# One more pipe step between scores and turned weights in the differential attention of the prompt

## The chip, the cores and the metric

One core of one Trainium2 chip runs the kernel. It has five engines with a queue of their own each: TensorE (PE; its weight loads are a row of their own, PEld), VectorE (DVE), ScalarE (ACT), GpSimd (POOL) and SyncE (SP), which here starts nearly all DMA transfers. The metric is the device time of one execution in microseconds. Before the change it is 935.0 us, the median of three runs (934.97 to 935.01).

## The reference

One decoder layer for a prompt of 512 rows and a group of 8 x 4 sample rows. The part that matters here is the differential attention of the mixer: 4 heads, each with two 64-wide query and key components and a 128-wide value. The prompt attends to itself causally, the sample rows attend to a paged cache of 256 rows.

```python
def diff_attend(q, k, v, mask, lam):
    s = jnp.einsum('bqhcd,bkhcd->bhcqk', q, k) * (DA_QK_DIM ** -0.5)
    s = jnp.where(mask[None, None, None], s, -jnp.inf)
    p = jax.nn.softmax(s, axis=-1)
    a = p[:, :, 0] - lam * p[:, :, 1]
    return jnp.einsum('bhqk,bkhd->bqhd', a, v)
```

Around it stand an mLSTM head group that reads the same normalised rows, an output projection of both, cross-attention into 256 memory tokens and a gated MLP with a short convolution. All of it is in fp32, large products as a sum of three products of rounded high and low halves.

## The kernel before

The kernel is one Python function that issues instructions through a tile framework. A tile comes from a pool: `npool` (`N(...)`, 5 buffers of 1032 columns), `t2p` (`T2(...)`, 8 buffers of up to 562 columns), `zp` (3 of 512), and in PSUM `psm` (`mmp(...)`, 5 banks) and `psa` (`at(...)`, 3 banks). The framework's scheduler, when the program is built, decides the order of the instructions on every engine from the order of the code, the free buffers and its own estimate of durations; semaphores are put in by it. At run time each engine takes its instructions strictly in that order. An instruction that uses a buffer again waits for the last reader of the tile that had it before.

The stage around the change runs from about 244 to 300 us. Two passes are woven into each other there.

The *prompt pass* has 16 tiles: tile i is row block b = i // 4 and head h = i % 4, and has (b + 1) * 128 keys. `da_soft(i)` (L1248) makes the scores of the two components with PE into two PSUM tiles `sda` (L1257; L1258 adds the mask with a bf16 product), takes their negated maxima with VectorE (`nm`, L1260), the exponentials and their sums with ScalarE into the weight tile `pda` (L1261), the factors `rc` with VectorE (L1263, L1264), and joins the components with one VectorE update (L1265). `da_turn(i)` (L1268) transposes the weights with PE into `tpa` (L1273) and copies them with ScalarE to `aT` (L1275). `da_av(i)` (L1279) multiplies them with the values on PE into `oda` (L1285), which ScalarE scales into `dao` (L1287). `da_end(i)` (L1289) closes a row block after its fourth tile: square on ScalarE (`dasq`, L1099), sum on VectorE (`dass`, L1101), a power and a product on GpSimd, transposes on PE (`dat`, L1106), and so on. `pipe` (L375) runs these as stages of a pipeline: its generator `prompt` makes one step per `next`, and in step t it issues stage s for tile t - s, the last stage first.

The *sample pass* goes over 8 batches. For each, SyncE loads two pages of cached keys into `wst` (256 KB each), PE transposes them in two groups of four (`tpk`, L1229, tiles of `psa`), ScalarE copies the first group and VectorE the second to `kT` (L1230), and PE makes the scores `ssc` of a pair of batches (L1242). VectorE and ScalarE make maxima and exponentials of them (L1052, L1053). After all eight, `sample_softmax` sums them with PE (`spa`, L1072) and ScalarE copies the sum (`spc`, L1074). Then eight loads of cached values (`vt`) and the products `ops` (L1341) follow. `out_gate` (L1029) runs in between: it transposes the mLSTM rows (`mlt`, L1039), gates them with VectorE into `mltm` (tiles of `t2p`, L1045; the sample rows also into `xts`, L296), and ScalarE and GpSimd split them into halves (L146, L147).

The generator `prompt` is stepped by hand from the sample pass: once per step of the loop over the key batches (10 steps), twice within `sample_softmax`, three times in the loop over the values, once after it, and four times between the first steps of the output projection (`proj`, lines L411 to L413).

Of the kernel before, what the change touches and what calls it, by code (L numbers as in the profile page):

```python
# [15 lines left out]
P = 128  # L16
# [6 lines left out]
H = 4  # L23
# [54 lines left out]
def kernel(ctx: ExitStack, tc: tile.TileContext, I, O):  # L78
# [23 lines left out]
    def S(shape, dt, name):  # L102
        return sp.tile(list(shape), dt, name=name, tag="S")

    def N(name, w=1024):
        return npool.tile([P, 1032], F32, name=name, tag="N")[:, :w]

    def T2(shape, name, dt=F32):
        return t2p.tile(list(shape), dt, name=name, tag="T2")
# [7 lines left out]
    def mmp(name="mm"):  # L117
        return psm.tile([P, 512], F32, name=name, tag="mm")

    def small(w, name, p=P):  # L120
        return sm.tile([p, w], F32, name=name, tag=name)
# [87 lines left out]
    def stage():  # L209
        return stg.tile([P, 1024], F32, name="wst", tag="st")  # L210
# [164 lines left out]
    def pipe(n, *stages):  # L375

        for t in range(n + len(stages) - 1):
            for s in reversed(range(len(stages))):
                if 0 <= t - s < n:
                    stages[s](t - s)  # L380
            yield
# [148 lines left out]
    for b in range(2):  # L530
        kept.append(norm_turn(xms[b], P, "g_mem_src", memT, b * P))
        if b == 0:

            t = turned[0].ins
            fill = mmp("fill")
            for _ in range(NFILL):
                with burst(t):
                    t = mm(fill, lhsT=warm[:, 0:P], rhs=warm, start=True, stop=True).ins
# [132 lines left out]
    for c0, c1 in HALF:  # L671
# [5 lines left out]
        t = T2([64, n], "gt")  # L677
# [253 lines left out]
    for g in range(2):  # L931
        for h in range(0, H, 2):
            t = stage().rearrange("p (j b e) -> p j b e", j=2, b=4)
# [38 lines left out]
    t = None  # L972
    for h in range(H):
        with burst(t):
            t = mm(pg[NS * h:NS * h + NS, P:2 * P + 1], lhsT=sm_t[:, h, :], rhs=vNs[:, h, :], start=True, stop=True).ins
    for h in range(H):
        with burst(t):
            t = mm(pg[NS * h:NS * h + NS, 4:12], lhsT=qT[:, h, SEQ:], rhs=nT[:, h, :], start=True, stop=True).ins
    for b in range(NB):
        for h in range(H):  # L980
            with burst(t):
                t = mm(pi[NS * h:NS * h + NS, 0:P], lhsT=qzm[:, 256 * h + b * NS:256 * h + (b + 1) * NS],
                       rhs=csts[b // 4, h][:, b % 4, :], start=(b == 0), stop=(b == NB - 1)).ins
# [226 lines left out]
    for b in range(4):  # L1210
        c = slice(b * P, b * P + P)
# [3 lines left out]
    kst, kts, pts, aTs, outs, rcs = {}, {}, {}, {}, {}, {}  # L1215
# [32 lines left out]
    def da_soft(i):  # L1248
        b, h = i // H, i % H
        c0 = b * P  # L1250
        nk = c0 + P
        pt = pts[i] = N("pda").rearrange("p (c k) -> p c k", c=2)
        nm = small(2, "nm")
        su = small(2, "su")
        sv = [mmp("sda")[:, :nk] for _ in range(2)]
        for c in range(2):
            mm(sv[c], lhsT=(dqz if c else dqT)[:, h, c0:c0 + P], rhs=dkT[:, h, 0:nk], start=True, stop=False)  # L1257
            mm(sv[c][:, c0:nk], lhsT=identb, rhs=cmaskb, start=False, stop=True)  # L1258
        for c in range(2):
            VRED(out=nm[:, c:c + 1], in_=sv[c], axis=AX.X, op=MAX, negate=True)  # L1260
            ACT(out=pt[:, c, :nk], in_=sv[c], func=AF.Exp, bias=nm[:, c:c + 1], accum_out=su[:, c:c + 1])  # L1261
        rc = sm.tile([P, 2], F32, name="rc", tag="rc", bufs=6)
        nc.vector.reciprocal(out=rc, in_=su)  # L1263
        VTS(out=rc[:, 1:2], in0=rc[:, 1:2], scalar1=su[:, 0:1], scalar2=nlam, op0=MUL, op1=MUL)  # L1264
        STT(out=pt[:, 0, :nk], in0=pt[:, 1, :nk], scalar=rc[:, 1:2], in1=pt[:, 0, :nk], op0=MUL, op1=ADD)  # L1265
        rcs[i] = rc
# [28 lines left out]


    W.nslots = 0
    prompt = pipe(4 * H, da_soft, lambda i: None, da_turn, da_av, da_end)
    sall = S([P, NB, 260], F32, "das")
    nm, su = small(NB, "snm"), small(NB, "ssu")  # L1300
    for t, _ in enumerate(pipe(NB, dk_load, dk_turn, dk_scores)):
# [45 lines left out]
                           start=False, stop=True).ins  # L1347

    for t, _ in enumerate(pipe(NB, dv_load, lambda b: None, dv_out)):
        if t % 2 == 0 and t > 2:  # L1350
            next(prompt, None)
        F.run(2)
    oS = T2([P, P], "daoS")
# [156 lines left out]
    def mk_scores(bs):  # L1510

        t = None
        ps = {b: at("ssc")[:, :256] for b in bs}
        for e in range(2):
            if e and bs[0] == 0:
                next(prompt)
                t = scored[0].ins
            for b in bs:
                o = ps[b][:, e * P:e * P + P].rearrange("p (h c t) -> p h c t", h=2, c=2)
                for c in range(2) if b < 3 else (None,):  # L1520
                    for j in range(8):
                        g = NS * (j % 4)
                        if c is None:
                            w, k = o[g:g + NS], view(kst[b][0], 512 * e + NS * j, [(256, 2), (DM, 2), (1, NS)])
                        else:
                            w, k = o[g:g + NS, :, c], view(kst[b][c], 512 * e + NS * j, [(256, 2), (1, NS)])
                        with burst(t):
                            t = mm(w, lhsT=qx[e][j // 4][:, j % 4, b].rearrange("p e g t -> p (e g t)"), rhs=k,
                                   start=(j < 4), stop=(j >= 4)).ins
        for b in bs:  # L1530
            nc.scalar.copy(out=sc[:, b], in_=ps[b])
        return t
# [66 lines left out]
    def steps():  # L1599

        for t in range(11):
            if t == AHEAD:
                ch_soft(t)
                yield
            if 0 <= t - 3 < 8:
                ch_out(t - 3)
            if 0 <= t - 2 < 8:
                ch_turn(t - 2)
            if t < 8 and t != AHEAD:
                ch_soft(t)  # L1610
            yield

    prompt = steps()
# [15 lines left out]
    for b in range(0, NB, 2):  # L1629
        t = mk_scores((b, b + 1))  # L1630
# [219 lines left out]
    for gi, js in enumerate(groups):  # L1850
# [6 lines left out]
        nk = len(js)  # L1857

        def one(b, ps, i, s, cs=slice(0, 512)):
            t = act[i // 2][:, i % 2]  # L1860
            st, en = i == 0, i == nk - 1
            if b == 4:
                return sample_mm(ps, [acs[i], acs[i + 1]], s[1], i == 0, i == nk - 2)
            s = s[0]
            c0 = b * P
            mm(ps, lhsT=t[:, 0, c0:c0 + P], rhs=s[:, 0, i % 2, cs], start=st, stop=False)  # L1866
            if js[i] == 21:
                return mm(ps, lhsT=t[:, 0, c0:c0 + P], rhs=s[:, 1, i % 2, cs], start=False, stop=en)
            mm(ps, lhsT=t[:, 0, c0:c0 + P], rhs=s[:, 1, i % 2, cs], start=False, stop=False)  # L1869
            return mm(ps, lhsT=t[:, 1, c0:c0 + P], rhs=s[:, 0, i % 2, cs], start=False, stop=en)  # L1870
# [29 lines left out]
        if not last:  # L1900
            behind = []
            for n0 in (0, 512):
# [4 lines left out]
                for i in range(nk):  # L1907
# [3 lines left out]
                    for b in range(4):  # L1911
                        t = one(b, ps[b], i, s)
# [14 lines left out]
        def chunk(b, n0):  # L1927
            while len(wd) < (nk // 2 if n0 == 0 else nk):
                wd.append(W.get())
            w = 256 if (b, n0) == (TORD[-1], 512) else 512  # L1930
            for o in range(0, 512, w):
                ps = mmp()[:, :w]
                for i in range(0, nk, 2 if b == 4 else 1):
                    t = one(b, ps, i, wd[(n0 and nk // 2) + i // 2], slice(o, o + w))
                add_y(b, ps, n0 + o, w)
            return t
# [39 lines left out]
        t = chunk(TORD[1], 0)  # L1976

        for n0 in (0, 512):
            with burst(t.ins):
                t = chunk(TORD[0], n0)  # L1980
# [79 lines left out]
```

## Time and profile before

| | |
|---|---|
| median of three runs | 935.0 us |
| profiled execution | 934.94 us |
| its span | 933.2 us |
| PE, busy of the span | 912.8 us (98%) |
| VectorE | 607.1 us (65%) |
| ScalarE | 377.9 us (40%) |
| GpSimd | 224.6 us (24%) |
| DMA, mean over the span | 140 GB/s |

The span reaches from the first to the last recorded instruction; the time of an execution is 1.74 us longer. Busy times are sums over the records of one engine. A row of a timeline merges instructions of one kind that follow each other: its length reaches from the first's start to the last's end, and since an instruction begins before the one in front has wholly ended, two rows can overlap. In brackets stands the idle time of the engine ahead of the row and the instruction that ended it. The page's slices of the span show a busy PE throughout, while VectorE and ScalarE are fullest in slices 10 to 12 of 40, which is the stage of this change.

### The profile page before, as it was taken

The page shows a single profiled execution, that of the slowest core. Times are in us where ns is not written, and L with a number is a line of the kernel's source. Part 1 is how long each engine was busy: PE and PEld are TensorE (multiplying, and loading weights), DVE is VectorE, ACT ScalarE, POOL GpSimd, SP SyncE. Part 2 cuts the span into 40 slices and gives each one's busy share as a digit, 9 for nine tenths or more (in the row PEclk, how much of TensorE's full clock was granted, in tenths as well). Part 3 has the DMA queues.
Part 4 walks back from the last instruction along what each step waited for, and adds up shares of the span by engine and source line. Part 5 has one row for each costly group of instructions (what it writes and reads, how often), then busy time and mean ns, then how long its engine had stood idle before and what let it go on. Part 6 is the DMA issues. An engine that isn't in the chain of part 4 may idle for free. (4 is left out here: it accounts for less than half of the span.)

```text
span 933.2 us, 17471 instructions
## 1 busy us (share of the span) xinstructions
PE 912.8 (98%) x6780; PEld 797.2 (85%) x6780; DVE 607.1 (65%) x1128; ACT 377.9 (40%) x728; POOL 224.6 (24%) x475
## 2 busy tenths in 40 slices
PE   8999999999999999999999999999999999999995
PEld 5899787879866778999877899889888998999974
DVE  5845144565888338677645878537748775776767
ACT  5645233344587437724534532422212222222232
POOL 6611000034442126581000652001000110110114
PEclk9999999999999999999999999999999999999998
DMA  9950023335780439966777632152154304413023
GB/s 288 316 182 6 1 91 139 91 102 164 234 299 17 136 113 293 302 213 228 284 240 201 199 105 62 31 174 69 27 136 136 91 4 127 124 47 91 25 94 118
DMA packets 120834, 130.59 MB, mean 140 GB/s; under 512 B 8599, under 2 KB 86264, under 8 KB 120752
## 3 DMA queue, kind: packets, MB, share of 16 engines
q1 hardware_dynamic: 114568, 125.96, 42.8%
q10 hardware_dynamic: 6184, 3.53, 1.3%
q8 instruction: 53, 0.87, 0.4%
q14 instruction: 29, 0.24, 0.1%
HBM read 112.54 MB, written 16.93 MB: 139 GB/s over the span
## 5 line engine op out<-in xcount | busy, mean ns | idle before, releaser
L485 PE MATMUL mm<-fT,wslot 128*128 128x256 f32 x1872 | 235.9, 288 | 0.0
L485 PEld LDWEIGHTS mm<-fT,wslot 128*128 128x128 f32 x1872 | 234.4, 188 | 1.8 <-issue 0.8
L146 ACT CAST wslot<-wst 128x1024 fp32r<-128x1024 f32 x125 | 130.4, 1050 | 255.7 <-issue 72.7
L147 DVE TENSOR_TENSOR wslot<-wst,wslot 128x1024 fp32r<-128x1024 f32 x125 | 154.2, 1239 | 76.5 <-ACT wslot L146 74.6
L1866 PE MATMUL mm<-wslot,act 128*128 128x512 f32 (+1 forms) x180 | 69.4, 387 | 0.0
L1869 PE MATMUL mm<-wslot,act 128*128 128x512 f32 (+1 forms) x172 | 67.1, 391 | 0.0
L1870 PE MATMUL mm<-wslot,act 128*128 128x512 f32 (+1 forms) x172 | 66.8, 392 | 0.0
L1768 POOL COPY cvo<-u 128x2 f32<-128x2 f32 x43 | 10.4, 242 | 216.0 <-DVE u L1766 216.0
L411 PE MATMUL mm<-wslot,hT 128*128 128x512 f32 x128 | 51.3, 402 | 0.0
L413 PE MATMUL mm<-wslot,hT 128*128 128x512 f32 x128 | 51.0, 400 | 0.0
L485 PE MATMUL mm<-hT,wslot 128*128 128x256 f32 (+1 forms) x384 | 51.0, 289 | 0.0
L412 PE MATMUL mm<-wslot,hT 128*128 128x512 f32 x128 | 50.9, 397 | 0.0
L1763 DVE TENSOR_TENSOR u<-mm,rsb 128x256 f32<-128x256 f32 x43 | 18.1, 424 | 48.8 <-PE mm L485 48.7
L485 PEld LDWEIGHTS mm<-hT,wslot 128*128 128x128 f32 x384 | 49.2, 188 | 0.5 <-issue 0.2
L1866 PEld LDWEIGHTS mm<-wslot,act 128*128 128x128 f32 x180 | 34.3, 191 | 7.9 <-issue 0.4
L1870 PEld LDWEIGHTS mm<-wslot,act 128*128 128x128 f32 x172 | 32.3, 188 | 6.9 <-issue 0.4
L1869 PEld LDWEIGHTS mm<-wslot,act 128*128 128x128 f32 x172 | 32.3, 188 | 6.8
L1780 ACT ACTIVATE c<-c 128x560 f32<-128x560 f32 x21 | 14.1, 672 | 56.8 <-DVE c L1774 56.7
L1774 DVE SCALAR_TENSOR_TENSOR c<-u,cvT,c 128x560 f32<-128x560 f32 x43 | 34.3, 799 | 0.9
L1773 DVE SCALAR_TENSOR_TENSOR c<-u,cvT,c 128x560 f32<-128x560 f32 x43 | 34.1, 794 | 0.2
L1881 DVE TENSOR_TENSOR yp<-mm,yp 128x512 f32<-128x512 f32 (+1 forms) x41 | 27.1, 674 | 4.8 <-PE mm L1870 4.6
L413 PEld LDWEIGHTS mm<-wslot,hT 128*128 128x128 f32 x128 | 24.1, 188 | 5.0
(497 smaller groups left out, 1858.0 us busy)
## 6 DMA issues: line engine op xcount, KB each, us to landing
wst<-in_w_up_dram SPq DMA_DIRECT2D x42, 512.0 KB
wst<-in_w_in_dram SPq DMA_DIRECT2D x28, 512.0 KB
wst<-in_w_down_dram SPq DMA_DIRECT2D x20, 512.0 KB
kvt<-in_cache_mem_k_dram SPq DMA_DIRECT2D x10, 512.0 KB
kvt<-in_cache_mem_v_dram SPq DMA_DIRECT2D x10, 512.0 KB
wst<-in_w_mk_dram SPq DMA_DIRECT2D x8, 512.0 KB
xb<-in_x_prompt_dram SPq DMA_DIRECT2D x8, 512.0 KB
wst<-in_cache_dk_dram SPq DMA_DIRECT2D x16, 256.0 KB
```

The lines of the kernel that those rows point to most:

```text
L146: nc.scalar.copy(out=hi, in_=src)
L147: (eng or nc.vector).tensor_tensor(out=lo, in0=src, in1=f32(hi), op=SUB)
L411: mm(ps[b], lhsT=xt.hi(k, c0, c0 + n), rhs=s[:, 0, kk, :], start=(k == 0), stop=False)
L412: mm(ps[b], lhsT=xt.hi(k, c0, c0 + n), rhs=s[:, 1, kk, :], start=False, stop=False)
L413: return mm(ps[b], lhsT=xt.lo(k, c0, c0 + n), rhs=s[:, 0, kk, :], start=False, stop=(k == nk - 1))
L485: mm(ps[i], lhsT=s[:, l, k, :], rhs=x(k, c0, c1), start=(k == 0 and j == 0), stop=(k == 7 and j == 2))
L1773: STT(out=c, in0=u[:, 1:EXT - 1], scalar=w[1], in1=c, op0=MUL, op1=ADD)
L1774: STT(out=c, in0=u[:, 0:EXT - 2], scalar=w[0], in1=c, op0=MUL, op1=ADD)
L1866: mm(ps, lhsT=t[:, 0, c0:c0 + P], rhs=s[:, 0, i % 2, cs], start=st, stop=False)
L1869: mm(ps, lhsT=t[:, 0, c0:c0 + P], rhs=s[:, 1, i % 2, cs], start=False, stop=False)
L1870: return mm(ps, lhsT=t[:, 1, c0:c0 + P], rhs=s[:, 0, i % 2, cs], start=False, stop=en)
L1881: VTT(out=y, in0=ps, in1=y, op=ADD)
```

## The change

Between `da_soft` and `da_turn` the pipeline of the prompt pass had one empty stage and now has two, so that it has six stages and 21 steps instead of five and 20. The loop over the cached values steps it at t = 2, 4, 6 and 8 instead of 4, 6 and 8. And the weight tiles of row blocks 0 and 1 (128 or 256 keys) come from `t2p` with just the columns they need instead of from `npool`.

```diff
-        pt = pts[i] = N("pda").rearrange("p (c k) -> p c k", c=2)
+        pt = pts[i] = T2([P, 2, nk], "pda") if b < 2 else N("pda").rearrange("p (c k) -> p c k", c=2)
...
-    prompt = pipe(4 * H, da_soft, lambda i: None, da_turn, da_av, da_end)
+    prompt = pipe(4 * H, da_soft, lambda i: None, lambda i: None, da_turn, da_av, da_end)
...
-        if t % 2 == 0 and t > 2:
+        if t % 2 == 0 and t > 0:
             next(prompt, None)
```

The scheduler makes another order of this stage; from some 330 us on all engines' queues read as before. On PE at the start of the stage, behind the scores of tiles 0 and 1, there stood (the numbers are those of the tile's allocation; `tpk` of 2618, 2664, 2670, 2736 and 2742 are the key transposes of batches 0 to 2, `tpa_2697` is the turn of tile 0, `sda_2704` and `sda_2705` the scores of tile 2):

```order
L1229 MATMUL tpk_2618<-cpk_87,wst_2572 128x128 x4
L1229 MATMUL tpk_2664<-cpk_87,wst_2624 128x128 x4
L1229 MATMUL tpk_2670<-cpk_87,wst_2624 128x128 x4
L1229 MATMUL tpk_2736<-cpk_87,wst_2676 128x128 x4
L1229 MATMUL tpk_2742<-cpk_87,wst_2676 128x128 x4
L1039 MATMUL mlt_2777<-cpk_87,mlh_1377 128x128 x4
L1273 MATMUL tpa_2697<-cpk_87,pda_2593 128x128
L1257 MATMUL sda_2704<-dkT_1303,dqT_1304 128x128
```

and now stands (2700 and 2701 are the scores of tile 2, 2732 and 2738 the transposes of batch 2, `ssc` the scores of batches 1 and 0):

```order
L1257 MATMUL sda_2700<-dkT_1303,dqT_1304 128x128
L1258 LDWEIGHTS cb_114
L1258 MATMUL sda_2700<-cb_114 128x128
L1229 MATMUL tpk_2618<-cpk_87,wst_2572 128x128 x4
L1229 MATMUL tpk_2664<-cpk_87,wst_2624 128x128 x4
L1229 MATMUL tpk_2670<-cpk_87,wst_2624 128x128 x4
L1257 MATMUL sda_2701<-dkT_1303,dqz_2557 128x128
L1258 LDWEIGHTS cb_114
L1258 MATMUL sda_2701<-cb_114 128x128
L1229 MATMUL tpk_2732<-cpk_87,wst_2676 128x128 x4
L1229 MATMUL tpk_2738<-cpk_87,wst_2676 128x128 x4
L1242 MATMUL ssc_2714<-kT_2662,qz_2553 32x260 x4
```

The scores of tile 2 moved in front of the first turn, one half ahead of the key transposes and one between them; the turn of tile 0 now follows the first pair of batch scores.

On VectorE, where the fourth and fifth tiles' scores meet the end of `out_gate` and the copies of batches 3 and 4, there stood (2831 and 2890 are the maxima of tiles 3 and 4, `pda_2701` and its factor `rc_2714` the weights of tile 2, `tpk_2855` and `tpk_2930` the second transposes of batches 3 and 4):

```order
L1260 TENSOR_REDUCE nm_2831<-sda_2833 128x1
L1260 TENSOR_REDUCE nm_2831<-sda_2834 128x1
L1045 TENSOR_TENSOR mltm_2817<-mlt_2815,soT_1306 128x128
L1265 SCALAR_TENSOR_TENSOR pda_2701<-pda_2701,rc_2714 128x128
L1230 COPY kT_2847<-tpk_2855 128x4x128
L296 COPY xts_2550<-mltm_2817 128x128
L1260 TENSOR_REDUCE nm_2890<-sda_2892 128x1
L1263 RECIPROCAL rc_2843<-su_2832 128x2
L1230 COPY kT_2922<-tpk_2930 128x4x128
```

and now stands (2883 are the maxima of tile 4, `tpk_2847` and `tpk_2923` the second transposes of batches 3 and 4, `pda_2822` the weights of tile 3):

```order
L1260 TENSOR_REDUCE nm_2883<-sda_2885 128x1
L1045 TENSOR_TENSOR mltm_2813<-mlt_2811,soT_1306 128x128
L1260 TENSOR_REDUCE nm_2883<-sda_2886 128x1
L1263 RECIPROCAL rc_2835<-su_2824 128x2
L296 COPY xts_2550<-mltm_2813 128x128
L1230 COPY kT_2839<-tpk_2847 128x4x128
L1264 TENSOR_SCALAR rc_2835<-rc_2835,su_2824,nlam_570 128x1
L1265 SCALAR_TENSOR_TENSOR pda_2822<-pda_2822,rc_2835 128x128
L1230 COPY kT_2915<-tpk_2923 128x4x128
```

The maxima of tile 4 and the copy `xts` moved in front of the copy of batch 3, and the update of tile 2's weights went ahead of all of these. On SyncE the sixth load of `w_out` went from between the two halves of the sixteen `cache_dv` loads to ahead of them.

## Rows read from the trace of the kernel before

**Rows 1.** The page's busy line: busy us, share of span, instructions.
```profile
PE 912.8 (98%) x6780; PEld 797.2 (85%) x6780; DVE 607.1 (65%) x1128; ACT 377.9 (40%) x728; POOL 224.6 (24%) x475
```

**Rows 2.** Table of waits, PE, whole span: us in total, times, longest.
```profile
PE tpa L1273 <- DVE pda L1265: 1.4, 2, 1.1
PE oda L1285 <- ACT aT L1275: 0.9, 1, 0.9
PE tpk L1229 <- ACT kT L1230: 0.5, 1, 0.5
PE tpk L1229 <- DVE kT L1230: 0.3, 1, 0.3
```

**Rows 3.** Window: busy of PE, PEld, DVE, ACT, POOL; clock; DMA; GB/s.
```profile
250.00:260.00 10.00, 9.70 (x95) 7.46 (x95) 9.93 (x30) 8.33 (x30) 6.25 (x9) 1.00 1.01 365
```

**Rows 4.** PE timeline: start, us, operation, count, [idle before, releaser].
```profile
245.28 0.44 PE L1257 MATMUL sda<-dkT,dqz 128*128 128x128 f32 x2
245.62 1.55 PE L1229 MATMUL tpk<-cpk,wst 128*128 128x128 f32 x12
247.48 0.66 PE L1229 MATMUL tpk<-cpk,wst 128*128 128x128 f32 x4 [0.32 <-DVE kT L1230]
248.66 0.66 PE L1229 MATMUL tpk<-cpk,wst 128*128 128x128 f32 x4 [0.52 <-ACT kT L1230]
...
256.32 0.33 PE L1273 MATMUL tpa<-cpk,pda 128*128 128x128 f32 x1 [0.30 <-DVE pda L1265]
...
256.98 1.04 PE L1229 MATMUL tpk<-cpk,wst 128*128 128x128 f32 x8
...
266.69 0.41 PE L1273 MATMUL tpa<-cpk,pda 128*128 128x128 f32 x2 [1.06 <-DVE pda L1265]
...
277.12 1.09 PE L1072 MATMUL spa<-das,csz 128*32 128x260 f32 x16
279.09 0.94 PE L1285 MATMUL oda<-dvN,aT 128*128 128x128 f32 x6 [0.88 <-ACT aT L1275]
...
285.39 1.95 PE L1341 MATMUL ops<-vt,daz 128*32 128x128 f32 x64
```

**Rows 5.** ScalarE timeline, start of the stage and beside PE's last wait.
```profile
247.59 0.19 ACT L1261 ACTIVATION_READ_ACCUMULATOR pda<-sda,nm 128x1 f32 x1
247.69 0.36 ACT L1261 ACTIVATE pda<-sda,nm 128x128 f32<-128x128 f32 x1
248.03 0.58 ACT L1230 COPY kT<-tpk 128x512 f32<-128x512 f32 x1
...
278.28 0.38 ACT L1074 COPY spc<-spa 128x260 f32<-128x260 f32 x1 [0.47 <-PE spa L1072]
```

**Rows 6.** VectorE timeline, the first four row blocks' steps.
```profile
248.17 0.17 DVE L1263 RECIPROCAL rc<-su 128x2 f32<-128x2 f32 x1 [0.74 <-ACT pda L1261]
...
255.22 1.04 DVE L1265 SCALAR_TENSOR_TENSOR pda<-pda,rc 128x128 f32<-128x128 f32 x1
256.19 0.68 DVE L1230 COPY kT<-tpk 128x512 f32<-128x512 f32 x1
256.79 0.70 DVE L296 COPY xts<-mltm 128x128 f32<-128x128 f32 x1
...
258.92 0.33 DVE L1265 SCALAR_TENSOR_TENSOR pda<-pda,rc 128x128 f32<-128x128 f32 x1
```

**Rows 7.** GpSimd timeline, the low halves of the gated mLSTM rows.
```profile
253.60 5.46 POOL L147 TENSOR_TENSOR mixT<-mltm,mixT 128x512 fp32r<-128x512 f32 x5 [1.53 <-ACT mixT L146]
```

**Rows 8.** Groups by form, 244 to 300 us: count, busy, mean ns, idle before.
```profile
L1099 ACT ACTIVATE dasq<-dao 128x512 f32<-128x512 f32 x3 | 1.9, 635 | 0.0
L1260 DVE TENSOR_REDUCE nm<-sda 128x1 f32<-128x256 f32 x8 | 3.2, 416 | 0.5 <-PE sda L1258 0.4
```

**Rows 9.** SyncE queue: loads of w_out and cache_dv.
```profile
269.47 0.39 SPq L231 DMA_DIRECT2D wst<-in_w_out_dram  x1
272.38 4.94 SPq L1094 DMA_DIRECT2D vt<-in_cache_dv_dram  x8
```

## The prediction

> **What bounds the kernel now.** I read the page's busy line first: PE is busy for 912.8 of the 933.2 us span, the next engine, VectorE, for 607.1 [rows 1]. So what PE does not wait for cannot be saved, and what it waits for mostly can. The table of PE's waits came second. Four of its entries belong to the code that the change touches: the turn of the weights (`tpa`) waits 1.4 us for VectorE's weights, the value product (`oda`) 0.9 us for ScalarE's copy of the turned weights, and the transposes of the cached keys (`tpk`) 0.5 and 0.3 us for their PSUM tiles [rows 2]. That is 3.1 us, all between 244 and 300 us. The third view, PE's timeline, puts places to them: 0.32 us before 247.48, 0.52 before 248.66, 0.30 before 256.32, 1.06 before 266.69 and 0.88 before 279.09, together 3.08 us [rows 4]. The fourth view says why a deeper pipe may not pay: from 250 to 260 us VectorE is busy 9.93 of 10 us, ScalarE 8.33, and PE 9.70 [rows 3]. There PE, VectorE and ScalarE are nearly one chain, and the granted clock is 1.00 (2.4 GHz) throughout.
>
> **The change, part by part.** No arithmetic is added or taken away. The third pipe step puts one more step between `da_soft(i)` and `da_turn(i)`: before, PE turns the weights of tile i right ahead of the scores of tile i+2, now of i+3. The pipe takes 21 steps for 20, and the extra `next` in the value loop gives it the place for the last one, so that the scores of the last tiles stand one step earlier there and the turns stand where they stood. The eight weight tiles of row blocks 0 and 1 take their memory from the pool of eight small tiles instead of the pool of five large ones. What moves is therefore the order on PE, VectorE and ScalarE, and I price it by walking the new order through the places where it has to wait, with the durations of the rows.
>
> *The start of the stage.* PE now issues the scores of a third tile before the first turn. Its first half, `sda_2700`, takes the fifth and last tile of the PSUM pool; half a tile steps 0.34 us (245.28 to 245.62), so the twelve transposes, 1.55 us, now end at 245.62 + 0.34 + 1.55 = 247.51 [rows 4]. The second half, `sda_2701`, needs a sixth tile. The first to come free is the one that ScalarE's first exponential has read, at 247.59 + 0.19 = 247.78 [rows 5]. PE idles 0.3 us. Then 0.34 us of scores and one group of four transposes, 0.66 us [rows 4], bring it to 248.8; the next group needs ScalarE's copy of `tpk_2664`, which began at 248.03 and now stands behind two more exponentials of 0.34 us each (247.69 to 248.03), so it ends at 248.03 + 0.68 + 0.58 = 249.29 [rows 5]. PE idles 0.5 us. Together 0.8 us for the 0.84 of before: a wait for one buffer in place of a wait for another. From the rows it can hardly be less than 0.5 (the table load ahead of the first exponential is the same) or more than 1.1 (another copy of 0.58 in front).
>
> *Row block 1 begins, about 257 us.* The wait of 0.30 us goes, since the weights that are turned there are a step older. Late next is the last group of four transposes of batch 4 (`tpk_2923`): it takes the PSUM tile that VectorE's copy of `tpk_2847` frees. The copy ended at 256.19 + 0.68 = 256.87 [rows 6]. In the new order it stands behind two more maxima of 256 columns, 0.42 us each [rows 8], and behind the `xts` copy, 0.70 us; the weights' update of 1.04 us at 255.22 comes earlier and may take the 0.33 us of the one at 258.92; and of VectorE's wait of 0.74 us before 248.17 some 0.4 us go, an estimate, because one more maximum stands ahead of it [rows 6]. That is 256.87 + 0.84 + 0.70 - 0.71 - 0.40 = 257.3. PE came to these transposes at 256.98 [rows 4]; in the new order it has by then the second half of a 256-wide score more (0.5 us), one value product and one turn less (0.4), and 0.3 us less idle, so 256.8 to 256.9. It idles 0.5 us. Lower end 0, if PE is later by that; upper end 1.2, if one more update takes 1.04 for 0.33. I take 0.5.
>
> *Before 267 us.* The wait of 1.06 us is of the kind that the step removes: the turn asked for an update that VectorE began at that moment, and now it asks for the one a step older. In its place the scores of row block 2 wait: their PSUM tiles come free behind exponentials, ScalarE has the square of the row block's output, 0.64 us [rows 8], between two of them, and VectorE's sum of that square holds the next maxima up. Ends 0 and the 1.06 that it replaces; I take 0.4, well below the row, since the square has an older exponential in front of it.
>
> *Before 279 us.* The value product behind `spa` waits for ScalarE's copy of the turned weights, which begins only after the copy `spc` at 278.28 [rows 5]. In the new order ScalarE still has `spc` and then that copy. The 0.88 us stay; ends 0 and 1.1.
>
> *What is hidden.* An exponential into one of the small tiles must wait until GpSimd has read that tile as a gated mLSTM row: five subtractions, 5.46 us from 253.60, so the first ends near 254.7 [rows 7], and by the same walk the first exponential that needs it comes near 256.7. Two microseconds cover it; without them the price is the remaining part of one subtraction, 1.1 us. On SyncE the sixth load of `w_out` (269.47) now stands ahead of the first eight `cache_dv` loads as well; the last of these were issued by 272.38 + 4.94 = 277.32 [rows 9], and PE reads the first at 285.39 [rows 4]. Eight microseconds cover a load of half a megabyte.
>
> The Trainium skill (SBUF — State Buffer, Who interferes with whom) says that a VectorE instruction with two SBUF inputs contends with a GpSimd instruction that reads SBUF, and that the later one blocks. The trace agrees in form: the 128-column update took 1.04 us inside GpSimd's stretch from 253.60 and 0.33 us at its end. By that rule the change would lose what it gains wherever an update newly falls beside GpSimd, which is the second rival below.
>
> **The sum.** New idle of PE: 0.3 + 0.5 + 0.5 + 0.4 + 0.9 = 2.6 us, for 3.08 before: 0.5 us less. Behind 300 us the engines stand in the order of before, and PE is the bound there, so this goes to the end. The profiled execution took 934.94 us (933.2 of span and 1.74 around it), against a median of 935.0. 934.94 - 0.5 = 934.4; I say 934.5, which is no change: this kernel's measurement tells 0.2% (1.9 us, so 933.1 and 936.9) from nothing. With each term at its ends (0.5 + 0 + 0 + 0, and 1.1 + 1.2 + 1.06 + 1.1 us) the time is 932.4 to 936.3.
>
> **Rivals.**
> 1. *The waits behind the first five microseconds all go.* For it: 1.36 us of the 3.08 are waits of a turn for weights, and a whole step more stands in front of every turn; PE being later than I have it by some tenths at each place would swallow the rest. Against it: VectorE at 9.93 of 10. Price: 0.8 us of idle stays, 2.3 us go: 932.7. Chance 0.30.
> 2. *VectorE becomes the bound* from 250 to 270 us. Mechanism: five subtractions of GpSimd lie beside VectorE's two-input updates, and the earlier start of the scores fills VectorE's last idle time, so that each lost tenth reaches PE through the transposes' PSUM tiles, of which there are three. It decides where the update of 1.04 us stays and one or more others become as slow, 0.71 us each. Three of them, at the transposes of batches 4 to 6, with the other terms at 0.3 + 0.5 + 1.06 + 0.9 and 0.5 + 3 x 0.71 at this one: 5.4 us of idle, 2.3 us more: 937.2. Chance 0.17.
> 3. *The change does not do what it says*: the order is made when the program is built, instruction by instruction, and may pull the turns back up. The order of the new kernel shows the turn of tile i behind the scores of tile i+2, so little speaks for it; 935.0. Chance 0.05.
> My forecast has the remaining 0.48, with a range of its own of 933.2 to 936.3.
>
> **How the numbers follow.** Faster by over 0.2% is rival 1: 0.30. Slower is rival 2: 0.17. Within 0.2%: 0.48 + 0.05 = 0.53. The range holds the forecast's and reaches to rival 1 at its price and a little below, and to near rival 2: 932.4 to 937.0.
>
> **What would show it.** Right: PE's timeline has a wait of `sda` for ScalarE's first exponential near 247.8 and one of `tpk` near 249; the waits of `tpa` for VectorE are gone; a wait of `tpk` for VectorE's copy stands near 257; the wait of `oda` for ScalarE behind `spa` is still there; PE's idle from 244 to 300 us is 2 to 4 us. Wrong: that idle is under 1.2 us (rival 1), or over 5 us with `tpk` waiting for VectorE more than twice (rival 2), or the times differ behind 330 us, where I have nothing moved.

## The result, and the profile of the changed kernel

The changed kernel takes 936.66 us (median of 20 runs, 935.44 to 937.77); the kernel before took 934.99 us in as many. The ratio is 1.0018, with a 95% interval of 1.0011 to 1.0024 (it is estimated apart from the medians and need not be their quotient): 1.7 us slower. I had forecast 934.5 us. The difference is inside the 0.2% that I had called no change, but more runs made the interval narrow enough to tell it from nothing, and its sign is not the one I forecast. The time lies inside the range that I gave (932.4 to 937.0 us), at its upper end.

The profiled execution took 936.22 us, 1.28 us more than that of before. One difference of two times says little about a place, so I measure a *stretch*: from the first scores of the prompt (`sda`, line 1257) to the start of the last third product of the output projection (line 413 on `mixT`). It holds everything that the change moves. It was 243.91 to 353.05 us in before, 109.1 us, and 244.95 to 355.69 us in after, 110.7 us: 1.6 us more, nearly the whole difference of the medians (1.67). The stretch begins 1.0 us later in after (PE waits longer for the first loads, at 11 to 17 us), and what lies behind it is 1.4 us shorter; the change edits neither.

The page's busy line, and the table of PE's waits (us in total, times, longest), answer to [rows 1, 2]:

```profile
PE 913.6 (98%) x6780; PEld 796.9 (85%) x6780; DVE 605.2 (65%) x1128; ACT 377.8 (40%) x728; POOL 222.5 (24%) x475
```

```profile
...
PE oda L1285 <- ACT aT L1275: 1.5, 1, 1.5
...
PE sda L1257 <- ACT pda L1261: 0.7, 1, 0.7
...
PE spa L1072 <- DVE csz L1065: 0.6, 1, 0.6
PE tpk L1229 <- ACT kT L1230: 0.5, 1, 0.5
PE tpk L1229 <- DVE kT L1230: 0.5, 1, 0.5
PE sda L1257 <- ACT das L1053: 0.4, 1, 0.4
```

The waits of `tpa` are gone, and six others stand there. PE's timeline of after puts places to them, against [rows 4]:

```profile
249.15 0.49 PE L1257 MATMUL sda<-dkT,dqz 128*128 128x128 f32 x2 [0.68 <-ACT pda L1261]
...
250.67 0.66 PE L1229 MATMUL tpk<-cpk,wst 128*128 128x128 f32 x4 [0.53 <-ACT kT L1230]
...
258.22 0.66 PE L1229 MATMUL tpk<-cpk,wst 128*128 128x128 f32 x4 [0.51 <-DVE kT L1230]
...
272.73 0.91 PE L1257 MATMUL sda<-dkT,dqT 128*128 128x384 f32 x2 [0.41 <-ACT das L1053]
...
277.59 1.08 PE L1072 MATMUL spa<-das,csz 128*32 128x260 f32 x16 [0.57 <-DVE csz L1065]
280.15 0.71 PE L1285 MATMUL oda<-dvN,aT 128*128 128x128 f32 x4 [1.47 <-ACT aT L1275]
```

Together 4.17 us, where before had 3.08: 1.09 us more. Half of the 4.17 lies at two neighbouring matmuls of the sample softmax, `spa` and the value product behind it. The engines' timelines say why. First VectorE of after, then GpSimd of after:

```profile
274.71 0.68 DVE L1108 TENSOR_TENSOR dtm<-dat,gT 128x512 f32<-128x512 f32 x1
...
275.90 0.16 DVE L1064 TENSOR_TENSOR scf<-scf,cpk 128x8 f32<-128x8 f32 x1
276.17 1.37 DVE L1065 TENSOR_TENSOR csz<-cpk,scf 128x128 f32<-128x128 f32 x1
277.46 0.54 DVE L1260 TENSOR_REDUCE nm<-sda 128x1 f32<-128x384 f32 x1
```

```profile
276.12 1.27 POOL L147 TENSOR_TENSOR mixT<-dtm,mixT 128x512 fp32r<-128x512 f32 x1 [3.27 <-ACT mixT L146]
277.33 1.81 POOL L1081 MEMSET daz<- 128x2048 f32 x1
```

The product that makes `csz`, the weights of `spa`, takes 1.37 us. In before the same product took 0.29:

```profile
275.94 0.29 DVE L1065 TENSOR_TENSOR csz<-cpk,scf 128x128 f32<-128x128 f32 x1
```

In after it begins 0.05 us behind a subtraction of GpSimd that takes 1.27 us. In before that subtraction (the low half of row block 0 in `mixT`) stood elsewhere:

```profile
270.54 1.55 POOL L147 TENSOR_TENSOR mixT<-dtm,mixT 128x512 fp32r<-128x512 f32 x1 [2.75 <-ACT mixT L146]
```

There an update of VectorE had begun 0.07 us ahead of it (270.47 us); the update took its usual 0.48 us, and it was the subtraction that took longer. With one more pipe step the row block is finished a step later, and its last work meets the sample softmax. So in after the next maximum of VectorE (277.46) is late by the same amount, the exponentials of ScalarE wait for it, and `spc` and `aT` stand behind these exponentials:

```profile
278.04 0.58 ACT L1261 ACTIVATE pda<-sda,nm 128x384 f32<-128x384 f32 x1 [1.17 <-DVE nm L1260]
...
278.88 0.58 ACT L1261 ACTIVATE pda<-sda,nm 128x384 f32<-128x384 f32 x1 [0.17 <-DVE nm L1260]
...
279.46 0.36 ACT L1074 COPY spc<-spa 128x260 f32<-128x260 f32 x1
279.71 0.38 ACT L1275 COPY aT<-tpa 128x256 f32<-128x256 f32 x1
```

The rest, 0.5 us, is no idle time: PE is *busy* for longer in the stretch. It lies behind 301 us, where I had said that nothing moves. PE's timeline of before, then of after, at the sample products of the projection (line 390; x is their number):

```profile
306.35 0.64 PE L390 MATMUL mm<-wst,xts 128*32 128x256 f32 x8
306.92 0.66 PE L1106 MATMUL dat<-cpk,dasq 128*128 128x128 f32 x4
307.51 1.50 PE L390 MATMUL mm<-wst,xts 128*32 128x256 f32 x24
```

```profile
308.57 1.93 PE L390 MATMUL mm<-wst,xts 128*32 128x256 f32 x30
310.43 0.66 PE L1106 MATMUL dat<-cpk,dasq 128*128 128x128 f32 x4
311.01 0.62 PE L390 MATMUL mm<-wst,xts 128*32 128x256 f32 x2
```

Both cut the run of 32 with four turns, but not at the same place: 2.14 us of sample products in before, 2.55 in after, which is 0.4 of the 0.5 us.

### The profile page after: what moved, and what is told of

Its sections match the earlier page's. It is cut to its first block, busy times and chain, and to the rows that moved or that the text cites. A ratio compares the mean times of both kernels' runs of the same rounds, so it can differ in the third digit from the quotient of the medians.

```text
span 934.4 us, 17469 instructions
## 1 busy us (share of the span) xinstructions
PE 913.6 (98%) x6780; PEld 796.9 (85%) x6780; DVE 605.2 (65%) x1128; ACT 377.8 (40%) x728; POOL 222.5 (24%) x475
```

## The experiments

All medians stand beside the kernel before, run on the same chip; the stretch is of one profiled execution each. "Large pool" means that no weights are in the small pool. In rows of kernels with added lines the line numbers stand some lines later; the operation and the names tell them.

| kernel | median us (before) | ratio, 95% interval | stretch us |
|---|---|---|---|
| before | 934.99 | 1 | 109.1 |
| after | 936.66 (934.99) | 1.0018, 1.0011 to 1.0024 | 110.7 |
| 1 after, no subtraction for block 0 | 935.18 (934.58) | 1.0007, 0.9998 to 1.0017 | 109.7 |
| 2 after, large pool | 935.03 (934.58) | 1.0006, 0.9998 to 1.0015 | 109.6 |
| 3 before, small pool | 935.39 (934.58) | 1.0011, 1.0002 to 1.0020 | 110.2 |
| 4 after, value loop as before | 943.99 (934.58) | 1.0106, 1.0091 to 1.0120 | 117.0 |
| 5 before, no subtraction for block 0 | 934.59 (934.76) | 0.9998, 0.9989 to 1.0007 | 109.2 |
| 6 after, one run of sample products | 935.58 (934.76) | 1.0011, 1.0002 to 1.0020 | 110.0 |
| 7 after, large pool and three repairs | 934.04 (934.76) | 0.9992, 0.9983 to 1.0001 | 108.6 |
| 8 before, two repairs | 933.65 (934.76) | 0.9983, 0.9972 to 0.9993 | 108.0 |
| 9 after, subtraction in four | 935.15 (934.34) | 1.0008, 0.9999 to 1.0018 | 109.9 |
| 10 after, sixth PSUM tile | 939.44 (934.34) | 1.0048, 1.0034 to 1.0062 | 113.3 |
| 11 after, three repairs | 934.62 (934.83) | 0.9999, 0.9985 to 1.0012 | 108.9 |
| 12 before, two repairs and dasq in four | 935.86 (934.83) | 1.0007, 0.9997 to 1.0017 | 110.3 |

**1 and 5: is it the collision?** The subtraction becomes a memset in the same place of GpSimd's queue, once in after and once, as a control, in before. This leaves the low half of row block 0 out of the output. The memset has no data to wait for and runs early, at 272.06 us in the first run.

```diff
-        put(mixT, 1, 0, 4, c0, n, tmp, nc.gpsimd)
+        if c0 == 0:
+            nc.scalar.copy(out=mixT.quad(1)[0][:, 0:4, c0:c0 + n], in_=tmp)
+            nc.gpsimd.memset(f32(mixT.quad(1)[1][:, 0:4, c0:c0 + n]), 0.0)
+        else:
+            put(mixT, 1, 0, 4, c0, n, tmp, nc.gpsimd)
```

> The changed kernel, but GpSimd's subtraction that makes the low half of the first row block's columns in mixT (1.27 us in the trace of after, beside the product that makes csz) is replaced by a memset: this part of the output is left wrong, all orders stay. Theory collision: the product that makes csz took 1.37 us in after and 0.29 us in before because it stood beside that subtraction; it falls back to 0.3 us, the wait of spa for it (0.57 us) goes, the wait of oda for aT falls from 1.47 to about 0.9 us, and the time falls by about 1.1 us, to some 935.6 us. Rival order: the product is slow for another reason or the chain behind it is late anyway (VectorE has dtm and two maxima ahead of it); waits within 0.2 us of those of after, and 936.7 us.

> A control: the kernel before with the same replacement as in the first experiment (GpSimd's subtraction for the first row block's low half in mixT becomes a memset, so this part of the output is left wrong). Theory collision: in before no product of VectorE that a matmul waits for stands beside that subtraction (csz took 0.29 us), so nothing is gained: 935.0 us (934.3 to 935.6), waits of TensorE as in before (3.1 us between 244 and 305 us). Rival: the subtraction costs wherever it stands, and its removal gains the same 1.0 us here, 933.9 us.

In the first run's timeline `csz` is back at 0.29 us, `spa` waits for nothing, and `oda` waits 1.11 us for 1.47; the other four waits are those of after to 0.01 us. VectorE, then PE:

```profile
275.44 0.29 DVE L1065 TENSOR_TENSOR csz<-cpk,scf 128x128 f32<-128x128 f32 x1
```

```profile
276.22 1.09 PE L1072 MATMUL spa<-das,csz 128*32 128x260 f32 x16
278.41 0.71 PE L1289 MATMUL oda<-dvN,aT 128*128 128x128 f32 x4 [1.11 <-ACT aT L1279]
```

The stretch is 1.0 us shorter, and the median stands 0.6 us above before instead of 1.7 (the intervals of the two ratios overlap, so the size rests on the rows). In the control nothing changes: 934.59 for 934.76 us, the waits of before. So it is the meeting that costs 1 us, not the subtraction.

**2, 3 and 4: which part of the change?** Each undoes or isolates one line of it.

```diff
 2:  pt = pts[i] = N("pda")...                                    (after, the pool's line of the change undone)
 3:  pt = pts[i] = T2([P, 2, nk], "pda") if b < 2 else N("pda")... (before, this line alone)
 4:  if t % 2 == 0 and t > 2:                                     (after, value loop undone)
```

> The changed kernel with the empty step and the earlier value-loop step, but all weights in the large pool (none in the small one). Theory extra step: scores that run one step earlier take the sixth PSUM tile and crowd VectorE and ScalarE at the sample softmax; the waits of sda (0.68 and 0.41 us in after) stay, and the time stays near 936.5 us, less up to 1.1 us if the product that makes csz no longer stands beside GpSimd's subtraction. Rival small pool: the cost comes with the small pool's tiles; then it is 935.0 us, with the waits of sda gone.

> The kernel before with only the weights of two row blocks in the small pool: no empty step, the value loop's steps as before. Theory extra step: no cost from the pool; the two waits of tpa for pda (1.4 us together) stay, no wait of sda, csz 0.3 us, and 935.0 us (934.3 to 935.7). Rival small pool: 936.7 us with new waits of sda or a later sample softmax.

> The changed kernel with the value loop's steps as before (not at its third turn), so that one more step of the prompt runs beside the output projection. Theory extra step: everything up to 282 us is as in after (waits of 0.7, 0.5, 0.5, 0.4, 0.6 and 1.5 us) and the time is 936.7 us (936.2 to 937.2). Rival value loop: the earlier step there is what costs; then 935.0 us, with the same waits ahead of 282 us and less after them.

The second lies at +0.5 us, and its interval includes 1. That is the rival's time, but not its mechanism, since the waits of `sda` stay, shorter (0.41 and 0.23 us). Its order has the first row block's turns (`dat`) 1.6 us earlier in the stretch, and GpSimd's subtraction meets a smaller product. VectorE there:

```profile
274.30 0.85 DVE L1064 TENSOR_TENSOR scf<-scf,cpk 128x8 f32<-128x8 f32 x1
275.25 0.29 DVE L1065 TENSOR_TENSOR csz<-cpk,scf 128x128 f32<-128x128 f32 x1
```

(0.85 us for 0.16, covered by the scores on PE.) The third was expected at before's time and is 0.8 us slower: the pool alone gives the key loop another order, in which PE waits 0.80 us for ScalarE's `kT`, 0.65 for an exponential ahead of `ssc` and 0.40 for `dasq`, while `csz` keeps its 0.29 us. So neither of my two readings of the third run held: the pool costs, but not with after's waits. The parts don't add up to the whole, because each has an order of its own.

The fourth missed both expectations: 9.4 us slower than before (four runs, 941.4 to 945.1 us; the profile is of the first of these). Up to 282 us its waits are those of after. Then one step more of the prompt stands beside the projection. There ScalarE's queue holds the casts of the next loads, which wait for their data until 313.59 us. The copy `aT` that PE needs comes only behind them and behind some smaller instructions, two of which wait for VectorE (0.95 and 0.49 us), at 319.71 us. ScalarE, then PE:

```profile
313.59 1.05 ACT L146 CAST memT<-wst 128x1024 fp32r<-128x1024 f32 x1 [7.13 <-DMA wst<-mem_d]
```

```profile
320.34 1.97 PE L1285 MATMUL oda<-dvN,aT 128*128 128x128 f32 x8 [5.13 <-ACT aT L1275]
```

PE waits once for 5.13 us. The step in the value loop is thus what makes the empty stage bearable at all; I had given it half a sentence.

**6: the cut run.**

```diff
+    run_of = [None]
...
-                    sample_mm(ps[b], [xt.sam(k), xt.sam(k + 1)], s[1], k == 0, k == nk - 2)
+                    with burst(run_of[0] if k and xt.name == "mixT" else None):
+                        run_of[0] = sample_mm(ps[b], [xt.sam(k), xt.sam(k + 1)], s[1], k == 0, k == nk - 2).ins
```

> The changed kernel with the 32 sample products of the first half of the output projection tied together into one run (in after one of them stands behind the four turns dat: 1.93 us and 0.62 us; in before 0.64 us and 1.50 us; the second half's run, in one piece, takes 1.93 us). Nothing else in the order of any engine moves. Theory: the second part of the loss, 0.59 us behind 301 us, is mostly that cut; the run takes 1.93 us in one piece, and the time falls by 0.5 to 0.6 us against after, to 936.1 us, with the six waits ahead of 305 us as in after. Rival: the second part is drift of other lines; the run is whole and the time stays at 936.7 us.

The run is whole, and the stretch 0.7 us shorter than that of after, with the six waits unchanged (0.68, 0.54, 0.52, 0.41, 0.57, 1.47):

```profile
308.18 1.93 PE L392 MATMUL mm<-wst,xts 128*32 128x256 f32 x32
310.05 0.66 PE L1109 MATMUL dat<-cpk,dasq 128*128 128x128 f32 x4
```

The sample products account for 2.55 - 1.93 = 0.62 us of it, and the value product behind the turns for 0.1 (1.16 us in after, 1.06 here). The time, 0.8 us above before, agrees; against after itself the intervals overlap, so the size rests on the rows.

**9: what kind of meeting?** The subtraction in four pieces, nothing else moved.

```diff
-        put(mixT, 1, 0, 4, c0, n, tmp, nc.gpsimd)
+        hi, lo = (t[:, 0:4, c0:c0 + n] for t in mixT.quad(1))
+        nc.scalar.copy(out=hi, in_=tmp)
+        for h in range(H):
+            nc.gpsimd.tensor_tensor(out=lo[:, h], in0=tmp[:, h], in1=f32(hi[:, h]), op=SUB)
```

> The changed kernel with GpSimd's subtraction of 128x512 for the low halves of mixT made in four of 128x128, one for each head; only GpSimd's rows differ. In after, VectorE's product for csz (0.29 us alone) began 0.05 us behind the subtraction and ended 0.15 us behind it; in before, an update of pda (0.47 us alone) that met a GpSimd product took 1.06 us and ended 0.28 us behind it. Theory hold: VectorE stands still for the GpSimd instruction that it meets, whatever its length; with pieces of some 0.4 us csz takes 0.5 to 0.8 us, spa's wait (0.57 us) goes, and the time falls by 0.4 to 0.8 us against after, to 936.1 us. Rival sharing: the two engines share bandwidth over the whole stretch; csz stays at 1.2 us or more as long as the four pieces last, and 936.7 us.

VectorE and GpSimd of this run:

```profile
275.36 0.56 DVE L1065 TENSOR_TENSOR csz<-cpk,scf 128x128 f32<-128x128 f32 x1
```

```profile
275.31 1.76 POOL L1112 TENSOR_TENSOR mixT<-dtm,mixT 128x128 fp32r<-128x128 f32 x4 [3.27 <-ACT mixT L1110]
```

GpSimd is busy for longer than in after (1.76 us for 1.27), and yet `csz` is through after 0.56 us. A share of bandwidth so small that 0.29 us became 1.37 in after would have kept it slow for nearly as long as the four pieces ran. It waits out the rest of one GpSimd instruction, then gets its turn. `spa` waits for nothing, `oda` 1.30 us, and the stretch is 0.8 us shorter. The Trainium skill (SBUF — State Buffer, Who interferes with whom) says that this contention is an exclusive lock; the traces of after and of this run agree (1.37 us behind one instruction of 1.27, 0.56 us behind one of four).

**10: term A, the sixth PSUM tile.**

```diff
-        sv = [mmp("sda")[:, :nk] for _ in range(2)]
+        sv = [(at if i == 2 and c else mmp)("sda")[:, :nk] for c in range(2)]
```

> The changed kernel with the second score tile of the third head taken from the other PSUM pool (three tiles, used there by the turns of the keys). Theory: term A is the sixth tile of the pool of five; the wait of sda for ScalarE's first exponential (0.68 us at 249 us) goes, unless the turns of the keys (tpk) now wait instead by as much; the stretch from 244 us to the end of the projection falls from 110.75 to between 110.1 and 110.75 us, and the time is 936.0 to 936.7 us. Rival: the first exponentials are late for VectorE's or ScalarE's sake, and the wait moves to the next matmul that needs them with its full 0.68 us.

The wait of `sda` falls from 0.68 to 0.25 us and the next `tpk` waits 1.41 us instead of 0.53: the wait has moved with interest, as the expectation feared. What was not expected is 2.5 us more in the stretch. The subtraction meets an update this time (1.67 us for some 0.6), the exponential behind it is late, and `oda` waits 2.35 us. After that wait the granted clock falls. From the end of the wait to the projection PE takes 22.9 us where after takes 21.2, which is 1.7 of the 2.5 us. First PE's timeline of this run, then windows of it (us, busy time of PE, PEld, DVE, ACT, POOL, clock, DMA share, GB/s):

```profile
279.97 1.02 PE L1285 MATMUL oda<-dvN,aT 128*128 128x128 f32 x4 [2.35 <-ACT aT L1275]
280.78 0.85 PE L1273 MATMUL tpa<-cpk,pda 128*128 128x128 f32 x3
281.42 1.49 PE L1257 MATMUL sda<-dkT,dqT 128*128 128x384 f32 x2
```

```profile
276.00:278.00 2.00, 1.62 (x19) 0.51 (x17) 2.00 (x3) 1.08 (x3) 1.52 (x2) 1.00 1.05 383
278.00:280.00 2.00, 0.03 (x1) 0.04 (x1) 1.19 (x5) 1.21 (x4) 1.53 (x1) 1.00 0.95 350
280.00:282.00 2.00, 2.00 (x8) 1.76 (x9) 0.73 (x2) 0.65 (x2) 0.00 (x0) 0.55 0.13 47
282.00:284.00 2.00, 2.00 (x7) 0.92 (x6) 0.95 (x2) 1.08 (x3) 0.00 (x0) 0.59 0.00 0
```

**7, 8, 11 and 12: do the repairs add up, and is there something better than both?** The repairs: the copy `spc` on VectorE, so that `aT` isn't behind it on ScalarE; the sample products in one run; for the collision, in 7 the rounding and subtraction of row block 0 queued behind the last `aT` of the two steps, in 11 the four pieces, in 12 `dasq` in four pieces.

```diff
-        nc.scalar.copy(out=a, in_=pa[:, :w])
+        VCP(out=a, in_=pa[:, :w])
...
 7:
+    with tc.issue_after(turned[0]):
+        put(mixT, 1, 0, 4, 0, P, kept[0], nc.gpsimd)
...
 12:
-        GTT(out=sq, in0=o, in1=rs.unsqueeze(2).broadcast_to([n, H, P]), op=MUL)
+        for h in range(H):
+            GTT(out=sq[:, h], in0=o[:, h], in1=rs[:, h:h + 1].broadcast_to([n, P]), op=MUL)
```

> The changed kernel with all weights in the large pool, and three repairs: the first row block's rounding and subtraction into mixT queued behind the two steps' copies aT, so that GpSimd's subtraction no longer stands beside the sample softmax; the copy spc on VectorE instead of ScalarE, so that aT isn't behind it; the sample products tied into one run. Theory: the wait of oda for aT, 1.17 us in the run with the large pool alone, falls to 0.1 to 0.5 us, the run of sample products takes 1.93 us, csz 0.29 us and the scf product 0.16 us; the stretch from the first scores to the end of the projection falls from 109.65 to some 108.2 us, and the time is 0.8 us under before, 934.1 us (933.4 to 934.9). Rival: the empty step moves work that costs elsewhere; as before or slower, 935.0 us or more.

> The kernel before (no empty step, no small pool) with two of these repairs: the copy spc on VectorE, and the sample products tied into one run. Theory: ScalarE copies aT at 277.8 instead of 278.55 us, the wait of oda (0.88 us) falls to about 0.1 us, the run of 0.64 and 1.50 us becomes 1.93 us; together 0.9 us less than before, 934.1 us. Rival: VectorE, with 8.4 of 10 us busy there, makes the next scores' maxima late by as much as ScalarE gains; 935.0 us.

> The changed kernel as it is (empty step, small pool) with three repairs: the subtraction in four pieces, the copy spc on VectorE, the sample products in one run. Theory: the losses add up, so the repairs do. The stretch from the first scores to the end of the projection was 110.75 us in after; the pieces gave 0.79 us, the one run 0.79 us, and the copy spc (0.26 us on ScalarE ahead of aT) should give 0.2 to 0.3 us: 108.9 us, against 109.1 of before, and 934.3 us (933.8 to 935.0), no change against before. Rival: the repairs overlap, or VectorE, with a copy more, is late for the next scores; 109.6 us or more, and 935.0 us or more.

> The kernel before with the copy spc on VectorE and the sample products in one run (which took 108.0 us from the first scores to the end of the projection), and GpSimd's product that scales a row block's output (dasq, 1.04 us) in four pieces, one for each head. Theory hold: before's longest wait, 1.06 us of tpa for pda, is an update that began 0.26 us behind such a product and took 1.06 us for 0.48; with pieces of 0.4 us it takes 0.7 us or less, the wait falls to 0.4 to 0.7 us, and the time is 0.3 to 0.6 us under the run without the pieces, 0.27% under before. Rival: the turns dat, which now wait for the pieces one by one, move between the scores and cost more than that; the waits move and the time is that of the run without the pieces or above it.

In run 11 the repairs add up as expected: 108.9 us were expected for the stretch and 108.9 measured, and no difference from before is left, 0.9999. Two of the three repairs also speed up before, though: run 8, which has just these two, takes 108.0 us. Against run 8 the extra step still costs 0.9 us of the stretch, and PE's waits are longer by as much: 3.17 us in run 11 (0.68, 0.54, 0.52, 0.41, and 1.02 of `oda`), 2.21 in run 8 (0.32, 0.52, 0.31 and 1.06). So the waits that the step brought in place of those of `tpa` are not repaired. Run 7 lies at 0.9992, with an interval that just includes 1; its stretch came to 108.6 and not 108.2 us, and its `oda` still waits 0.68 us where 0.1 to 0.5 were expected. Run 8 beats both kernels: 0.9983 of before, with an interval that excludes 1. Its wait of `oda` is gone altogether; its PE timeline at the place of [rows 4]:

```profile
278.30 1.09 PE L1075 MATMUL spa<-das,csz 128*32 128x260 f32 x16
279.42 0.94 PE L1288 MATMUL oda<-dvN,aT 128*128 128x128 f32 x6
```

Run 12 missed its expectation, and with it falls my reading of before's longest wait. The update that met `dasq` is back at 0.48 us, but `tpa` still waits, for the update ahead of it, which takes 0.47 us in both kernels:

```profile
266.71 0.41 PE L1277 MATMUL tpa<-cpk,pda 128*128 128x128 f32 x2 [1.05 <-DVE pda L1269]
```

Splitting `dasq` also let its turns slip between other matmuls, and two new waits of 0.79 us for `aT` came (279.03 and 317.03 us).

## Why the prediction was wrong

The forecast was 2.6 us of idle time for 3.08; it is 4.17, just above the 2 to 4 us that I had named as a sign of being right. Term by term (expected, measured):

- **The waits of `tpa` go:** they went. All 1.36 us.
- **A, the third head's second score tile:** 0.3, measured 0.68. The walk was right (PE stops for the first exponential). PE came when I said; but ScalarE's table load, which I took to be where it was, begins 2.39 us behind the first scores instead of 2.12, since it now waits for VectorE's first maximum (below, in before and in after).
- **B, the transposes behind ScalarE's copy:** 0.5, measured 0.53. A and B together are 1.21 us, above the 1.1 that I had called the most.
- **C, the last transposes of batch 4:** 0.5, measured 0.51, at the place and for the releaser that I named. The size is partly luck: VectorE's wait at the start did not shrink by 0.4 us (it is 0.81 for 0.74), and the `xts` copy took 0.26 us for the 0.70 that I had counted; the two errors cancel.
- **D, the scores of row block 2:** 0.4, measured 0.41. The wait is one for a PSUM tile behind a ScalarE exponential as I had it, but it is the sample's exponential (`das`), and the place is 5 us later than the wait that it was to replace.
- **E, the value product behind `spa`:** 0.9, measured 1.47, above its upper end of 1.1; and ahead of it `spa` waits 0.57 us for `csz`, which I had not at all. This is the step that failed. I carried ScalarE's order over to the new kernel and left VectorE's out of it: `csz` stands behind `dtm` and beside a subtraction that the extra step has moved there. Run 1 gives 0.93 us of these 2.04 to the meeting. In it `oda` still waits 1.11 us: an exponential (277.15 to 277.73 us) stands ahead of `spc`, at a place where ScalarE in before had only `spa` to wait for [rows 5].

The table loads of term A:

```profile
246.03 1.28 ACT L1261 ACT_TABLE_LOAD   x1
```

```profile
247.34 1.28 ACT L1261 ACT_TABLE_LOAD   x1 [0.29 <-DVE nm L1260]
```

VectorE's wait and the `xts` copy of term C, in after, against [rows 6]:

```profile
249.48 0.17 DVE L1263 RECIPROCAL rc<-su 128x2 f32<-128x2 f32 x1 [0.81 <-ACT pda L1261]
...
257.31 0.26 DVE L296 COPY xts<-mltm 128x128 f32<-128x128 f32 x1
```

A, `spa` and E miss by 0.38, 0.57 and 0.57 us, B to D by 0.05: the whole 1.57 us. **The sentence that nothing moves behind 300 us** failed too: the orders agree only from some 330 us on. That is a second term, which I had put at nothing, of 0.5 us; 0.4 of it is that one or two of 32 sample products stand behind the turns `dat` instead of 24. I had looked at waits alone, and this is a busy engine that is busy for longer.

**Rival 2** had the right mechanism at the wrong place. A two-input instruction of VectorE beside GpSimd did cost 1 us, but at 276 us and for one instruction; in the stretch from 250 to 260 that I had named, VectorE is *less* busy than in before (against [rows 3]), and its updates there take 0.34 and 0.47 us where one took 1.04 [rows 6]:

```profile
250.00:260.00 10.00, 8.96 (x88) 6.72 (x87) 9.66 (x34) 8.37 (x30) 5.54 (x7) 1.00 0.95 337
```

So 936.7 us is near that rival's price of 937.2 by another sum. The rival spoke of the stretch where the trace of before showed such a meeting. The question to ask was where the *moved* GpSimd instructions would land. **Rival 1** (all waits behind the first five microseconds go) and **rival 3** (the change does nothing) are refuted by PE's timeline. **The covers held:** no wait for a small tile behind GpSimd's rows, and none of PE for a `cache_dv` load, shows in after.

What stays open: why what follows the stretch took 1.4 us less in after. Times that differ behind 330 us were one of my signs of being wrong. One wait of 1.2 us for `ql` in the memory attention, present in before and absent in after, varies between 0 and 1.6 us over these profiles, and I found no part of the change that sets it.

## What to carry to other kernels

When a step moves, move all of its tail with it in thought: the instructions of the engines that nobody waits for land somewhere too, and a GpSimd instruction that falls beside the one two-input VectorE product that a matmul waits for can cost nearly its whole length (1.08 of 1.27 us here). An order made by a program moves matmuls far from the edit, so compare busy time per line as well as waits. And before making a pipeline deeper, look for what its waits stand behind: moving one copy to another engine and tying one run together gave 0.9983 where the extra step gave 1.0018.

## What the runs showed of the hardware

- A VectorE product with two inputs in SBUF waits out the rest of the GpSimd subtraction that it meets (1.37 us for 0.29 beside one of 1.27 us; 0.56 beside the first of four). Where VectorE began first, the subtraction took longer instead (1.55 us in before). A memset of GpSimd held nothing up: in run 2 `csz` takes its usual 0.29 us wholly beside the one of 1.81 us that begins at 275.06 us.
- In run 10 PE, busy for 1.62 of the 2 us ahead, waited 2.35 us; that was followed by 4 us with a granted clock of 0.55 to 0.59 (nearly all at the lower level, 1.2 of 2.4 GHz); the same two products of 384 columns took 1.49 us there and 0.81 in after. The wait of 5.13 us in run 4 was followed by a clock of 0.57, the wait of 1.47 us in after by 1.00. Windows of run 4, then of after:

```profile
320.00:324.00 4.00, 3.66 (x15) 3.46 (x16) 1.09 (x2) 1.83 (x5) 0.00 (x0) 0.57 0.26 92
```

```profile
280.00:284.00 4.00, 3.85 (x26) 3.13 (x27) 2.67 (x7) 2.95 (x15) 0.74 (x2) 1.00 0.15 57
```

- Four turns that cut a run of 32 products of 32 rows cost 0.21 us behind the eighth and 0.62 us ahead of the last one or two, each against the run in one piece (1.93 us).
